# First stage of a decoder block on one core: where the first activation rows and the first columns of w_ada land, in which order their loads are issued, and a modulation summed in two halves

## The chip, the cores and the metric

One NeuronCore of one Trainium2 chip runs the whole kernel. Its five engines each work through their own instruction list in order and wait for one another by semaphores: TensorE (PE), VectorE (DVE), ScalarE (ACT), GpSimd (POOL) and SyncE (SP), whose instructions here are nearly all transfers between the chip's main memory and the core's SBUF. The metric is the device time of one execution in microseconds (us), as a median over runs.

## The reference, cut to what matters

One layer of a decoder with 1024 tokens of width 1024. The part that the change touches is the beginning, the first norm with its modulation:

```python
cond = jax.nn.silu(c)
mod = cond @ w_ada[l] + b_ada[l]
sh_a, sc_a, gt_a, sh_f, sc_f, gt_f = jnp.split(mod[:, None, :], 6, axis=-1)
h = rms_norm(x, norm_mix_g[l]) * (1.0 + sc_a) + sh_a
proj = h @ w_in[l]
```

`w_ada` is 1024 x 6144. Its first 2048 columns give the shift `sh_a` and the scale `sc_a` that the first norm needs. Everything behind `proj` (an attention branch, an mLSTM branch, their gated merge, then a squared-ReLU MLP) is the same before and after the change and takes all but the first 60 us or so of the run.

## The kernel before, in words

The 1024 tokens are eight tiles `j` of 128 rows. For each tile there are the steps `x_square` (load `xt`, 128 x 1024 in fp32, 512 KB, and sum its squares on ACT), `x_rms` (the power -0.5 on DVE and POOL), `x_turn` (scale the rows on DVE, transpose the tile on PE against the identity `ident`) and `x_out` (copy the transposed halves out of PSUM into `xT`, one half by ACT, one by DVE). A loop over `j` runs these staggered: tile `j` is squared while tile `j-1` is turned and tile `j-2` copied out.

Beside it `load_mod(q, j)` loads rows `j*128` to `j*128+127` of the first 2048 columns of `w_ada` for half `q` of the features (`wa`, two stretches of 512 columns, 512 KB) and adds `wa * cond` into an accumulator `macc` on DVE: one `tensor_scalar` for `j` = 0 and seven `scalar_tensor_tensor` after it. When all eight are in, `modulate(q)` sums `macc` over its 128 partitions by eight small matmuls against a matrix of ones and adds the bias (`shg`), from which `gsc` is made. The steps that `modulate` returns then apply scale and shift to `xT` and split the result into a rounded part `hh` (ACT) and the rest `hl` (DVE), which together are `hT`. `first_unit` multiplies `hT` by the first weights of `w_in` (`w_hi`, `w_lo`; PSUM tile `ops`) and by a small matrix of gate columns (`wgs`, PSUM tile `gps`). Half 0 of the features goes first; while its steps run, the eight `load_mod(1, j)` are woven in between.

In the loop's pass `j == 2` a set of small parameters is loaded: 67 rows of gains and biases into `parr` (five loads, from 0.5 to 24 KB), the two other constant matrices into `ksq` (`ones` is one of them), the gate columns `wg` (32 KB in pieces of 32 bytes) and two bias rows `gb`. PE turns `parr` into columns `par`; ACT and DVE make `wgs` out of `wg`.

What sets the order: a scheduler at build time lays every engine's list out; instructions wrapped in `pin(...)` keep the order in which the program states them among themselves. All loads of this stage are issued by SP, in SP's list order. Each load is given one of eight completion counters in rotation (DMAHW0 to DMAHW7), and a load whose counter still has an unfinished load on it holds SP up until that one has landed, so SP has at most eight loads under way. Tiles come from pools with a fixed number of buffers per tag: "v" and "e" have four each, "x" has four large ones of 128 x 8 x 512.

## Time and profile before

| | |
|---|---|
| median of 3 runs | 2036.21 us (2036.16 to 2036.49) |
| profiled execution, its own time | 2033.65 us |
| span of its trace | 2031.9 us |
| PE busy | 1970.7 us, 97% |
| DVE busy | 1636.7 us, 81% |
| ACT busy | 1053.0 us, 52% |
| moved by DMA | 307.21 MB |

The span is the stretch from the first to the last recorded instruction. Times in the trace count from the start of the span. In rows of the timeline the two first numbers are start and duration in us, then come engine, line of the kernel, operation, the tile written and the tile read, shapes and a count; a bracket gives how long the engine had been idle before the row and what released it. SPq is SP's list of transfers: its rows are the issue of a transfer, not its landing. The view of windows gives busy time of each engine in a stretch, then the granted TensorE clock (1.00 is full), the share of the DMA engines and GB/s.

### The profile page before, as it was taken

The numbers are of one execution on the slowest core, as the hardware profiler recorded it, in microseconds if no ns is written. First come the engines' busy times: TensorE is split into PE (matmuls) and PEld (weight loads), VectorE is DVE, ScalarE is ACT, GpSimd is POOL, SyncE is SP. The second block draws the span as 40 slices with busy tenths as digits, with TensorE's granted clock in tenths as the row PEclk, the third lists the DMA queues.
The fourth block names the chain that finished last, engine by engine and source line by source line (L and its number), as shares of the span: only waits on it lengthen the run. The fifth ranks groups of instructions, "written<-read, shape, count | busy, mean of one in ns | idle before, by whom it ended". The sixth has DMA issues, their size and how long they took to land.

```text
span 2031.9 us, 30206 instructions
## 1 busy us (share of the span) xinstructions
PE 1970.7 (97%) x11193; PEld 1709.9 (84%) x11193; DVE 1636.7 (81%) x2883; ACT 1053.0 (52%) x1983; POOL 55.8 (3%) x150
## 2 busy tenths in 40 slices
PE   5999999999999999999999889999999999999999
PEld 5999998888888899999999668877788888888887
DVE  7977668988766568999978757999867668999896
ACT  5523224544566557777766534546645545433332
POOL 0000000000011000000000100000000000000000
PEclk7999999999999999999999999999999999999999
DMA  8376633335665442322223875603446446755531
GB/s 285 107 221 205 203 113 119 104 104 181 194 169 170 121 116 63 84 63 84 63 83 87 288 263 186 202 22 127 147 145 218 165 151 227 276 181 156 165 114 73
DMA packets 205386, 307.21 MB, mean 151 GB/s; under 512 B 14435, under 2 KB 115454, under 8 KB 205238
## 3 DMA queue, kind: packets, MB, share of 16 engines
q1 hardware_dynamic: 202358, 295.84, 45.9%
q0 software_dynamic: 2880, 9.44, 1.2%
q8 instruction: 88, 1.44, 0.3%
q14 instruction: 60, 0.49, 0.1%
HBM read 212.19 MB, written 84.64 MB: 146 GB/s over the span
## 4 chain that ended last, share of the span: by engine, by line
PE 77%; DVE 8%; DMA 6%; issue 4%; ACT 4%; POOL 1%; SPq 0%; DVEq 0%; POOLq 0%; ACTq 0%
PE cps L329 18%; PE pa L329 10%; PE pc L329 10%; PE pb L329 10%; PE pd L329 5%; PE ps L167 4%; PE ps L166 4%; PE ps L168 4%; PE lg L1220 3%; PE pv L1273 2%; DMA ex<-ea_d 1%; PE ops L586 1%; PE tp L1253 1%; DMA w<-in_w_ff_dram 1%; DMA xt<-in_x_dram 1%
## 5 line engine op out<-in xcount | busy, mean ns | idle before, releaser
L329 PE MATMUL cps<-t_op,s_op 128*128 128x512 f32 x2016 | 466.8, 393 | 2.1 <-DVE t_op L139 1.8
L329 PEld LDWEIGHTS cps<-t_op,s_op 128*128 128x128 f32 x2016 | 377.9, 188 | 88.1 <-DVE t_op L139 2.1
L321 ACT ACTIVATE w_op<-w_st 128x512 fp32r<-128x512 f32 (+1 forms) x197 | 135.9, 705 | 196.2 <-PE pb L329 60.0
L139 DVE TENSOR_TENSOR w_op<-w_st,w_op 128x512 fp32r<-128x512 f32 (+1 forms) x197 | 150.0, 780 | 27.2 <-ACT w_op L321 25.3
L166 PE MATMUL ps<-w_hi,hT 128*128 128x256 f32 x512 | 146.5, 286 | 0.0
L167 PE MATMUL ps<-w_lo,hT 128*128 128x256 f32 x512 | 145.9, 285 | 0.0
L168 PE MATMUL ps<-w_hi,hT 128*128 128x256 f32 x512 | 145.6, 284 | 0.0
L321 ACT ACTIVATE s_op<-act 128x1024 fp32r<-128x1024 f32 x56 | 59.0, 1053 | 149.0 <-PE cps L329 109.5
L1230 ACT ACTIVATE ee<-ee,mneg 128x256 f32<-128x256 f32 (+7 forms) x128 | 98.4, 770 | 12.8 <-DVE mneg L1226 12.5
L1220 PE MATMUL lg<-kb,qe 128*128 128x512 f32 (+3 forms) x384 | 96.0, 357 | 5.2 <-DVE mneg L1226 3.5
L329 PE MATMUL pc<-bt,w_op 128*128 128x512 f32 x384 | 96.7, 399 | 2.4 <-ACT w_op L321 1.4
L167 PEld LDWEIGHTS ps<-w_lo,hT 128*128 128x128 f32 x512 | 97.6, 191 | 1.4 <-issue 0.9
L166 PEld LDWEIGHTS ps<-w_hi,hT 128*128 128x128 f32 x512 | 97.6, 191 | 0.5
L168 PEld LDWEIGHTS ps<-w_hi,hT 128*128 128x128 f32 x512 | 97.6, 191 | 0.3
L329 PE MATMUL pa<-b,w_op 128*128 128x512 f32 x384 | 93.5, 393 | 0.3 <-DVE w_op L139 0.3
L329 PEld LDWEIGHTS pc<-bt,w_op 128*128 128x128 f32 x384 | 71.8, 190 | 22.3 <-DVE w_op L139 5.3
L329 PEld LDWEIGHTS pa<-b,w_op 128*128 128x128 f32 x384 | 72.2, 189 | 15.6 <-DVE w_op L139 0.7
L317 DVE TENSOR_TENSOR acc<-cps,acc 128x512 f32<-128x512 f32 x108 | 71.5, 682 | 11.0 <-PE cps L329 11.0
L1226 DVE CUSTOM_DVE_ANT_0 ee<-lg,bs 128x512 f32<-128x512 f32 (+4 forms) x128 | 69.7, 558 | 8.8 <-PE lg L1220 7.8
L139 DVE TENSOR_TENSOR s_op<-act,s_op 128x1024 fp32r<-128x1024 f32 x56 | 68.2, 1218 | 6.6 <-ACT s_op L321 6.5
L1220 PEld LDWEIGHTS lg<-kb,qe 128*128 128x128 f32 x384 | 60.2, 189 | 14.3 <-DVE mneg L1226 8.5
L329 PE MATMUL pa<-hT,w_op 128*128 128x512 f32 x264 | 64.1, 392 | 0.0
(416 smaller groups left out, 4746.1 us busy)
## 6 DMA issues: line engine op xcount, KB each, us to landing
w_st<-in_w_in_dram SPq DMA_DIRECT2D x72, 512.0 KB, 4.0
act<-act_d SPq DMA_DIRECT2D x56, 512.0 KB, 4.3
w_st<-in_w_ff_dram SPq DMA_DIRECT2D x36, 512.0 KB, 4.1
crow<-in_w_ada_dram SPq DMA_DIRECT2D x32, 512.0 KB, 4.6
w<-in_w_ff_dram SPq DMA_DIRECT2D x32, 512.0 KB, 4.7
act_d<-s SPq DMA_DIRECT2D x40, 256.0 KB, 2.0
act_d<-c SPq DMA_DIRECT2D x33, 256.0 KB, 2.0
act_d<-m SPq DMA_DIRECT2D x33, 256.0 KB, 2.0
```

The source lines that it names most:

```text
L139: return (nc.gpsimd if pool else nc.vector).tensor_tensor(dst, src, hi.bitcast(F32), op=ALU.subtract)
L166: nc.tensor.matmul(o, lhsT=ah, rhs=bh, start=first, stop=False)
L167: nc.tensor.matmul(o, lhsT=ah, rhs=bl, start=False, stop=False)
L168: nc.tensor.matmul(o, lhsT=al, rhs=bh, start=False, stop=last)
L317: (nc.gpsimd if pick(pool, n) else nc.vector).tensor_tensor(o, a, b, op=ALU.add)
L321: nc.scalar.activation(dst[0], src, AF.Copy)
L329: nc.tensor.matmul(ps, lhsT=p, rhs=q, start=first and k == 0 and r == 0, stop=k == 3 and r == 2, skip_group_check=True,)
L586: nc.tensor.matmul(o, lhsT=a[ra], rhs=w[rb][:, k, :], start=k == 0 and ra == rb and j % 2 == 0, stop=k == KT - 1 and ra == 1, skip_group_c ...
L1220: nc.tensor.matmul(lg[:, 0:max(256, w)], lhsT=hd["q"][hf][e][:, r, q4 * P:(q4 + 1) * P], rhs=hd["k"][e][:, c0:c0 + max(256, w)], start=r = ...
L1226: nc.vector.tensor_tensor_reduce(ee[:, c0:c0 + w], lg[:, 0:w], hd["bs"][:, n - c0 - w:n - c0][:, ::-1], -0.125, first, ALU.add, ALU.min, last,
L1230: nc.scalar.activation(ee[:, 0:n], ee[:, 0:n], AF.Exp, bias=mneg[:, e:e + 1], scale=-1.0, accum_out=ssum[:, e:e + 1])
L1273: nc.tensor.matmul(pv[:, 0:256], lhsT=pts[kk // 4][r][:, (kk % 4) * P:(kk % 4 + 1) * P], rhs=v, start=kk == 0 and r == 0, stop=kk == qi an ...
```

## The change

The tiles `xt` are no longer taken one by one from the tag "v". Two large tiles of the pool of `hT` are taken ahead of `hT`, and each holds four of the eight tiles of x side by side. The eight loads of `wa` for half 0 get a buffer each (four of "e", four of "v"), and so do those for half 1 after them. Loading is taken out of `x_square` and `load_mod` into `x_load` and `fetch_mod`, all of it pinned, and stated ahead of the loop: x of tiles 0 to 3, then in turns `wa` and x of tiles 4 to 7, then the last four `wa`. `modulate` does its eight matmuls in two groups of four, each with its own bias addition and its own `gsc`.

```diff
+    xst = [xp.tile([P, KT, 512], F32, name=f"xst{i}", tag="x").rearrange("p k c -> p (k c)") for i in range(2)]
     hT = ActX("hT")
...
+    def x_load(j):
+        xs[j] = xst[j // 4][:, j % 4 * D:(j % 4 + 1) * D]
+        pin(nc.sync.dma_start(xs[j], x2[j * P:(j + 1) * P, :]))
+
     def x_square(j):
-        xt = xs[j] = wt("v", [P, D], "xt")
-        nc.sync.dma_start(xt, x2[j * P:(j + 1) * P, :])
+        xt = xs[j]
...
+    def fetch_mod(q, j):
+        was[q, j] = wt("ev"[j % 2], [P, 2, 512], "wa")
+        src = w_ada[0, j * P:(j + 1) * P, 0:2048].rearrange("p (s c) -> p s c", s=2)
+        pin(nc.sync.dma_start(was[q, j], src[:, :, q * 512:(q + 1) * 512]))
+
     def load_mod(q, j):
-        wa = wt("e", [P, 2, 512], "wa")
-        src = w_ada[0, j * P:(j + 1) * P, 0:2048].rearrange("p (s c) -> p s c", s=2)
-        nc.sync.dma_start(wa, src[:, :, q * 512:(q + 1) * 512])
+        wa = was.pop((q, j))
...
     def modulate(q):
-        ks = slice(q * 4, q * 4 + 4)
         mod = bank("pa", "mod")
-        for s in range(8):
-            nc.tensor.matmul(
-                mod[:, 2 * s:2 * s + 2], lhsT=mods[q][:, s // 4, (s % 4) * P:(s % 4 + 1) * P], rhs=ones[:, 0:2],
-                start=True, stop=True,
+
+        for k in range(0, 4, 2):
+            for s in (k, k + 1, 4 + k, 5 + k):
+                nc.tensor.matmul(
+                    mod[:, 2 * s:2 * s + 2], lhsT=mods[q][:, s // 4, (s % 4) * P:(s % 4 + 1) * P], rhs=ones[:, 0:2],
+                    start=True, stop=True,
+                )
+            kq = slice(q * 4 + k, q * 4 + k + 2)
+            nc.vector.tensor_tensor(
+                shg[:, :, kq], mod[:, 0:16].rearrange("p (s k r) -> p s k r", s=2, r=2)[:, :, k:k + 2, 0],
+                bada[:, 0:2, kq], op=ALU.add,
             )
-        nc.vector.tensor_tensor(
-            shg[:, :, ks], mod[:, 0:16].rearrange("p (s k r) -> p s k r", s=2, r=2)[:, :, :, 0],
-            bada[:, 0:2, ks], op=ALU.add,
-        )
-        nc.vector.scalar_tensor_tensor(gsc[:, ks], shg[:, 1, ks], 1.0, gmix[:, ks], op0=ALU.add, op1=ALU.mult)
+            nc.vector.scalar_tensor_tensor(gsc[:, kq], shg[:, 1, kq], 1.0, gmix[:, kq], op0=ALU.add, op1=ALU.mult)
...
     ada = [ada_unit(u) for u in range(8)]
+    for j in range(4):
+        x_load(j)
+    for j in range(4):
+        fetch_mod(0, j)
+        x_load(4 + j)
+    for j in range(4, NT):
+        fetch_mod(0, j)
     for j in range(NT + 3):
...
     ahead()
+    for j in range(NT):
+        fetch_mod(1, j)
     weave(modulate(0), [lambda j=j: load_mod(1, j) for j in range(NT)])
```

Three places of the engines' lists. The words in brackets name what an instruction waits for: DMAHW with a number is the completion counter of a load, an engine's name is that engine. First SP's list, from the third tile of x on, as it stood before:

```order
L500 DMA xt_150<-in_x_dram 128x1024
L101 DMA parr_169<-in_norm_mix_g_dram 8x128
L101 DMA parr_169<-in_b_ada_dram 48x128
L101 DMA parr_169<-in_norm_ffn_g_dram 8x128
L101 DMA parr_169<-in_mhn_g_dram 2x128 [waits DMAHW0_49]
L101 DMA parr_169<-in_subln_g_dram 1x128 [waits DMAHW1_49]
L1393 DMA ksq_87<-in_k_sq_dram 128x2x128 [waits DMAHW2_49]
L1396 DMA wg_180<-in_w_in_dram 128x8x8 [waits DMAHW3_49]
L1400 DMA gb_126<-in_b_igate_dram 128x4 [waits DMAHW4_49]
L1400 DMA gb_126<-in_b_fgate_dram 128x4 [waits DMAHW5_49]
L500 DMA xt_187<-in_x_dram 128x1024 [waits DMAHW6_49]
L526 DMA wa_206<-in_w_ada_dram 128x2x512 [waits DMAHW7_49]
```

and as it stands now, from the last tile of x on (`xst1` is the second large tile):

```order
L501 DMA xst1_108<-in_x_dram 128x1024 [waits DMAHW5_49]
L531 DMA wa_145<-in_w_ada_dram 128x2x512 [waits DMAHW6_49]
L531 DMA wa_147<-in_w_ada_dram 128x2x512 [waits DMAHW7_49]
L531 DMA wa_149<-in_w_ada_dram 128x2x512 [waits DMAHW0_49]
L531 DMA wa_151<-in_w_ada_dram 128x2x512 [waits DMAHW1_49]
L101 DMA parr_189<-in_norm_mix_g_dram 8x128 [waits DMAHW2_49]
L101 DMA parr_189<-in_b_ada_dram 48x128 [waits DMAHW3_49]
L101 DMA parr_189<-in_norm_ffn_g_dram 8x128 [waits DMAHW4_49]
L101 DMA parr_189<-in_mhn_g_dram 2x128 [waits DMAHW5_49]
L101 DMA parr_189<-in_subln_g_dram 1x128 [waits DMAHW6_49]
L1411 DMA ksq_87<-in_k_sq_dram 128x2x128 [waits DMAHW7_49]
L1414 DMA wg_200<-in_w_in_dram 128x8x8 [waits DMAHW0_49]
```

Before, the small parameters stood behind three tiles of x; now they stand behind all eight tiles of x and all eight `wa` of half 0. The counter DMAHW0 that `wg` waits for is held by `wa_149`, the seventh of the eight `wa`.

Second, ACT's list at the place where `wgs` is made, before:

```order
L502 ACTIVATE jk_152,ssx_115<-xt_150 128x1024 [waits DMAHW4_49]
L518 COPY xT00_118<-tp_138 128x4x128 [waits PE_49]
L1397 ACTIVATE wgs_181<-wg_180 128x8x8 [waits DMAHW3_49]
L502 ACTIVATE jk_189,ssx_115<-xt_187 128x1024 [waits DMAHW6_49,Activation_49]
L518 COPY xT00_118<-tp_155 128x4x128 [waits PE_49]
```

and now:

```order
L506 ACTIVATE jk_172,ssx_117<-xst0_107 128x1024 [waits DMAHW4_49]
L522 COPY xT00_120<-tp_160 128x4x128 [waits PE_49]
L1415 ACTIVATE wgs_201<-wg_200 128x8x8 [waits DMAHW0_49]
L506 ACTIVATE jk_207,ssx_117<-xst0_107 128x1024 [waits DMAHW5_49,Activation_49]
L522 COPY xT00_120<-tp_175 128x4x128 [waits PE_49]
```

The place is the same in both: `wgs` stands between the squares of tile 2 and tile 3. On DVE and PE too the instructions that read `wg` and `parr` stand where they stood, ahead of the scaling and the transposes of tile 2.

Third, DVE's list around `modulate(0)`, from the last but one `scalar_tensor_tensor` of half 0 on, before:

```order
L533 SCALAR_TENSOR_TENSOR macc_208<-wa_316,cond_97,macc_208 128x1024 [waits DMAHW1_49,DVE_49]
L533 SCALAR_TENSOR_TENSOR macc_208<-wa_319,cond_97,macc_208 128x1024 [waits DMAHW2_49,DVE_49]
L139 TENSOR_TENSOR w_lo_323<-w_st_324,w_hi_322 128x1024 [waits DMAHW3_49,Activation_49]
L543 TENSOR_TENSOR shg_116<-mod_332,par_170 128x2x4 [waits PE_49]
L547 SCALAR_TENSOR_TENSOR gsc_117<-shg_116,par_170 128x4 [waits DVE_49]
L139 TENSOR_TENSOR w_lo_323<-w_st_328,w_hi_322 128x1024 [waits DMAHW4_49,Activation_49]
L531 TENSOR_SCALAR macc_348<-wa_346,cond_97 128x1024 [waits DMAHW5_49]
L139 TENSOR_TENSOR hT10_108<-xT00_118,hT00_107 128x2x256 [waits Activation_49]
L533 SCALAR_TENSOR_TENSOR macc_348<-wa_354,cond_97,macc_348 128x1024 [waits DMAHW6_49,DVE_49]
L139 TENSOR_TENSOR hT10_108<-xT00_118,hT00_107 128x2x256 [waits Activation_49]
```

and now:

```order
L139 TENSOR_TENSOR w_lo_317<-w_st_318,w_hi_316 128x1024 [waits DMAHW3_49]
L542 SCALAR_TENSOR_TENSOR macc_224<-wa_151,cond_97,macc_224 128x1024 [waits DMAHW1_49,DVE_49]
L139 TENSOR_TENSOR w_lo_317<-w_st_322,w_hi_316 128x1024 [waits DMAHW4_49,Activation_49]
L554 TENSOR_TENSOR shg_118<-mod_342,par_190 128x2x2 [waits PE_49]
L558 SCALAR_TENSOR_TENSOR gsc_119<-shg_118,par_190 128x2 [waits DVE_49]
L554 TENSOR_TENSOR shg_118<-mod_342,par_190 128x2x2 [waits PE_49]
L558 SCALAR_TENSOR_TENSOR gsc_119<-shg_118,par_190 128x2 [waits DVE_49]
L540 TENSOR_SCALAR macc_358<-wa_326,cond_97 128x1024 [waits DMAHW6_49]
L139 TENSOR_TENSOR hT10_110<-xT00_120,hT00_109 128x2x256 [waits Activation_49]
L542 SCALAR_TENSOR_TENSOR macc_358<-wa_328,cond_97,macc_358 128x1024 [waits DMAHW1_49,DVE_49]
L139 TENSOR_TENSOR w_op_608<-w_st_586,w_op_608 128x1024 [waits DMAHW1_49,Activation_49]
L139 TENSOR_TENSOR hT10_110<-xT00_120,hT00_109 128x2x256 [waits Activation_49]
```

One of the two `w_lo` (1024 columns) has moved ahead of the last accumulation into `macc`, and the second ahead of `shg`. The `w_op`, which stood behind all accumulations of half 1, now stands ahead of the second subtraction for `hT`; ACT's rounding of the same `w_op` has moved likewise, ahead of the second rounding of `hT`. On PE the second group of four `mod` matmuls waits for DVE.

More of the change, by code (lines that the diff above doesn't have):

```diff
@@ L520, in x_out @@
             ))
+    was = {}
+    def fetch_mod(q, j):
+        was[q, j] = wt("ev"[j % 2], [P, 2, 512], "wa")
+        src = w_ada[0, j * P:(j + 1) * P, 0:2048].rearrange("p (s c) -> p s c", s=2)
+        pin(nc.sync.dma_start(was[q, j], src[:, :, q * 512:(q + 1) * 512]))
     def load_mod(q, j):
-        wa = wt("e", [P, 2, 512], "wa")
-        src = w_ada[0, j * P:(j + 1) * P, 0:2048].rearrange("p (s c) -> p s c", s=2)
-        nc.sync.dma_start(wa, src[:, :, q * 512:(q + 1) * 512])
+        wa = was.pop((q, j))
         if j == 0:
```

## The prediction

> **What bounds the kernel now.** I read the shares of the page first, then the stretch that the change touches.
>
> ```profile
> PE 1970.7 (97%) x11193; PEld 1709.9 (84%) x11193; DVE 1636.7 (81%) x2883; ACT 1053.0 (52%) x1983; POOL 55.8 (3%) x150
> PE   5999999999999999999999889999999999999999
> ```
>
> TensorE is busy 97% of the span, and of the 40 slices only the first (0 to 50.8 us) is half empty. The edit lies in that slice, so the stage that ends with PE's unbroken run is what counts. The view of windows shows where that run begins.
>
> ```profile
> 15.00:20.00 5.00, 1.30 (x8) 0.90 (x8) 4.18 (x8) 2.77 (x6) 1.10 (x2) 0.79 1.03 407
> 20.00:25.00 5.00, 3.65 (x16) 3.14 (x16) 4.95 (x8) 2.98 (x7) 1.10 (x2) 0.50 1.04 397
> 40.00:45.00 5.00, 4.92 (x21) 4.40 (x21) 5.00 (x6) 4.90 (x11) 0.00 (x0) 0.50 0.70 206
> 45.00:50.00 5.00, 5.00 (x36) 4.10 (x36) 5.00 (x7) 4.91 (x11) 0.00 (x0) 0.98 0.88 279
> ```
>
> From 45 us on PE is busy for the whole window, at full clock (0.98); before 40 us it is not, and from 20 to 45 us its clock is granted at half speed. In 15 to 25 us DVE is nearly full (4.18 and 4.95 of 5 us), and the transfers run at 407 and 397 GB/s. So behind 15 us DVE and the transfers bind. The chain that ends last names the links:
>
> ```profile
> 9.14 4.66 DMA xt<-in_x_dram
> 13.89 1.16 ACT jk L502 x2
> 33.84 3.56 PE mod L539 x16
> 37.88 1.10 ACT xT L560 x2
> 42.21 4.46 PE ops L586 x24
> ```
>
> x of tile 3 and its squares, the eight `mod` matmuls, the first modulation on ACT, and from 42.21 us only PE. Whatever moves 42.21 moves the end, so I work out that time.
>
> **The change, part by part.** The place where it decides is not x or `wa` but the small loads that now stand behind them. Before, they went out early:
>
> ```profile
> 3.40 0.34 SPq L101 DMA_DIRECT2D parr<-in_b_ada_dram  x1
> 6.93 0.39 SPq L1396 DMA_DIRECT2D wg<-in_w_in_dram  x1
> 10.11 0.26 ACT L1397 ACTIVATE wgs<-wg 128x64 fp32r<-128x64 f32 x1
> 15.74 0.74 DVE L531 TENSOR_SCALAR macc<-wa,cond 128x1024 f32<-128x1024 f32 x1
> 18.57 1.28 DVE L533 SCALAR_TENSOR_TENSOR macc<-wa,cond,macc 128x1024 f32<-128x1024 f32 x1
> 19.76 0.75 DVE L511 TENSOR_SCALAR xt<-xt,ssx 128x1024 f32<-128x1024 f32 x1
> 20.61 0.68 DVE L518 COPY xT<-tp 128x512 f32<-128x512 f32 x1
> 21.21 1.28 DVE L533 SCALAR_TENSOR_TENSOR macc<-wa,cond,macc 128x1024 f32<-128x1024 f32 x1
> 20.65 1.94 PE L514 MATMUL tp<-ksq,xt 128*128 128x128 f32 x8 [2.15 <-DVE xt L511]
> ```
>
> `wg` was issued at 6.93, and ACT made `wgs` at 10.11 without a wait. ACT's list, like DVE's and PE's, still has the readers of `wg` and `parr` ahead of the work on tile 2 or 3. Those engines take their lists in order, so squares of tiles 3 to 7, scalings of tiles 2 to 7 and all eight accumulations stand behind `wg`.
>
> *When does `wg` land now?* The rows are two of ACT's, one of SP's waits, and two of the view of transfers from 0 to 60 us (slices of 1.5 us; the last number of the last row is the time from issue to landing).
>
> ```profile
> 5.66 1.06 ACT L502 ACTIVATE jk<-xt 128x1024 bf16<-128x1024 f32 x1 [1.75 <-DMA xt<-in_x_dram]
> 8.28 1.06 ACT L502 ACTIVATE jk<-xt 128x1024 bf16<-128x1024 f32 x1 [0.19 <-DMA xt<-in_x_dram]
> ...
> SPq L1396 <- DMA xt<-in_x_dram: 0.9, 1, 0.9
> ...
> GB/s 0 87 232 410 376 117 20 75 352 377 406 425 397 403 395 396 389 389 385 365 348 371 385 385 355 37 0 198 201 288 244 299 291 307 275 39 0 0 0 11
> parr<-in_b_ada_dram SPq DMA_DIRECT2D x1, 24.0 KB, 5.1
> ```
>
> (a) ACT starts on the first x at 5.66 and on the third, released by its landing, at 8.28: 1.31 us for each 512 KB, 400 GB/s; from 12 to 36 us the slices hold 348 to 425. (b) SP really stops on a full set of counters: it held `wg` for 0.9 us until a tile of x had landed. (c) A 24 KB load (`b_ada`, issued at 3.40) took 5.1 us, until 8.5, just behind the third x at 8.28: small loads do not overtake. In the new list x and `wa` make 16 loads of 512 KB. The first lands at 5.66, the fifteenth (`wa_149`, whose counter `wg` needs) at 5.66 + 14 x 1.31 = 24.0, the sixteenth at 25.3. `wg` is issued at 24.0 and not sooner whatever the queue does. It cannot land before the 128 KB of `ksq`, which stand behind the sixteenth: 25.3 + 0.33 = 25.6. In the run before the geometry was the same (one 512 KB load and `ksq` still ahead), and it was there 3.2 us after issue (10.11 - 6.93) at the latest: 27.2. I take **26.8**, nearer that row. At 425 GB/s all through, the fifteenth would land 1.1 us sooner, at 365 GB/s 1.8 us later. Nothing below 25 is left, since 15 loads must be in.
>
> By the Trainium skill ("DMA: Bandwidth & Descriptors", Specifications) a core's share of main memory is about 358 GB/s; the 16 loads would then take 23.4 us instead of 21.0 and the sum below would be 2.4 us higher, an estimate from that page. This trace moves 397 to 407 GB/s in 15 to 25 us, so I stay with the trace.
>
> *From `wg` to the second accumulation.* `wgs` on ACT is done at 27.0, the squares of tile 3 take 1.16, to 28.15. Then DVE copies tile 1 (0.68) and starts the first accumulation at 28.85 (0.74), the scaling of tile 3 at 29.5 (0.75) and the copy of tile 2 at 30.35 (0.68; tile 2 is scaled by 28.2, and its transposes take 1.94, to 30.2), and the second accumulation at 30.95. Before it was at 18.57. From there DVE is the limit in both, 2.64 us a tile (21.21 - 18.57); that x and `wa` are all there no longer helps. **Shift so far +12.4.** The early loads of x are worth nothing in it: tile 3 no longer waits for its transfer (4.66 in the chain), but for `wg`.
>
> *Around `mod`.*
>
> ```profile
> 31.14 2.60 DVE L533 SCALAR_TENSOR_TENSOR macc<-wa,cond,macc 128x1024 f32<-128x1024 f32 x2
> 33.65 1.22 DVE L139 TENSOR_TENSOR w_lo<-w_st,w_hi 128x1024 fp32r<-128x1024 f32 x1
> 37.62 0.16 DVE L547 SCALAR_TENSOR_TENSOR gsc<-shg,par 128x4 f32<-128x4 f32 x1
> 37.71 1.22 DVE L139 TENSOR_TENSOR w_lo<-w_st,w_hi 128x1024 fp32r<-128x1024 f32 x1
> 39.67 0.69 DVE L139 TENSOR_TENSOR hT<-xT,hT 128x512 fp32r<-128x512 f32 x1
> ```
>
> Before, the two `w_lo` (1.22 each, some 1.1 where the next instruction overlaps the end) ran beside the `mod` matmuls and behind `gsc`. Now one stands ahead of the last accumulation, nothing hides it: **+1.1**. The last accumulation, which ended at 33.74 (31.14 + 2.60), ends at 33.74 + 12.4 + 1.1 = 47.25, and `mod` starts at 47.35 (33.84 before). The first four matmuls take half of 3.56, to 49.1, the first `gsc` is there at 49.5, 2.15 us behind the start of `mod` where it was 3.94 (37.78 - 33.84). But the second group waits for DVE's first `shg` (0.25), its `gsc` comes at 51.5, and DVE runs the first accumulation of half 1 (0.74) and `hT`'s first subtraction (0.69, to 52.8) only after it. ACT's second modulation waits for it too (1.10, 51.55 to 52.65).
>
> *The moved `w_op`.*
>
> ```profile
> 52.55 1.06 ACT L321 ACTIVATE w_op<-w_st 128x1024 fp32r<-128x1024 f32 x1 [1.38 <-DMA w_st<-in_w_in_dram]
> 53.65 1.22 DVE L139 TENSOR_TENSOR w_op<-w_st,w_op 128x1024 fp32r<-128x1024 f32 x1 [0.56 <-ACT w_op L321]
> ...
> w_st<-in_w_in_dram SPq DMA_DIRECT2D x4, 512.0 KB, 6.9
> ```
>
> Before, its rounding on ACT (1.06) and subtraction on DVE (1.22) fell into gaps, with 1.38 and 0.56 us of idle time before them. Now they stand ahead of the second `hT` parts: ACT 52.6 to 53.65, rounding of `hT` to 54.25; DVE second accumulation from 52.7 (1.28), `w_op` 53.9 to 55.1, subtraction of `hT` to 55.7. Its load waits until the first `w_lo` has freed a buffer (46.1); with the 6.9 us that such loads took it lands at 53.0, so at most 0.4 us more. PE's unbroken run starts at 55.75: 8.4 us behind the start of `mod`, just as before (42.21 - 33.84 = 8.37). Pairing gains about 1.1 us, the moved `w_op` loses it: **0**, between -1.1 (if `w_op` were hidden) and +0.4.
>
> *Later.*
>
> ```profile
> 54.55 1.84 PE L539 MATMUL mod<-ksq,macc 128*128 128x2 f32 x16
> ```
>
> For half 1 the second group of `mod` again waits for DVE, now on PE's own path: **+0.25**. DVE's rest of half 1, six accumulations and six subtractions, takes 6 x (1.28 + 0.69) = 11.8 us at most, to 67.5; PE reaches `mod` 12.3 us after the start of its run (54.55 - 42.21), at 68.1. So DVE's work stays hidden, by 0.6 us.
>
> *Clock.*
>
> ```profile
> 44.09 0.41 PE L586 MATMUL ops<-w_lo,hT 128*128 128x256 f32 x1
> 44.73 0.41 PE L586 MATMUL ops<-w_lo,hT 128*128 128x256 f32 x1
> 45.32 0.28 PE L586 MATMUL ops<-w_lo,hT 128*128 128x256 f32 x1
> 45.68 0.28 PE L586 MATMUL ops<-w_lo,hT 128*128 128x256 f32 x1
> ```
>
> Three matmuls of 256 columns lie between each two of these rows: 0.21 us for one at half speed, 0.12 at full. The rise came near 45.1, 2.9 us into the unbroken run, and PE had worked for most of the 2.5 us ahead of it. Now it works in bits between 51.4 and 55.7. If the rise comes up to 2.5 us later in the run, that costs up to 2.5 x (1 - 0.12/0.21) = 1.1; I take **+0.3**, nearer to no difference.
>
> The page "TensorE: Matmul & The Clock Gate" of the Trainium skill (Part 1) gives full speed after about 3.4 us of sustained work, by a free-running window. By it the rise would come some 3.4 us into the run instead of 2.9, +0.2 as an estimate; the rise in this trace, 2.9 us into the run and 5.4 us behind PE's first matmul of the stage, does not contradict it.
>
> **Sum:** 12.4 + 1.1 + 0 + 0.25 + 0.3 = 14.05. The profiled execution, 2033.65 us around a span of 2031.9, becomes 2047.7 around 2045.9. The median lies 2.6 above that execution: 2036.2 + 14.05 = **2050.3**.
>
> **Rivals.** *A: The small loads stall nothing*, because they overtake the large ones. Then `wgs` is made near 10.1 as before, tile 3 (landed at 5.66 + 3 x 1.31 = 9.6) is squared by 11.5, the first accumulation runs at 12.3 and the second 2.1 later at 14.4 instead of 18.57; less the exposed `w_lo` the gain is 4.2 - 1.1 = 3.1, time 2033.1. For it speaks that x of tile 3 and the fourth load behind it do wait in the chain now; against it row (c), and row (b) above all, since a load that SP has not issued cannot overtake. 4%.
>
> *B: The delay is taken up later.* PE is idle for 61 us of the span (2031.9 - 1970.7). If 10 to 13 us of this were waits for transfers that run ahead on their own, these would shrink, and 1 to 4 us would be left: 2037 to 2040. Against it, PE's waits from 38 to 200 us:
>
> ```profile
> PE ops L586 <- ACT hT L563: 2.3, 1, 2.3
> PE pc L329 <- DVE m L317: 1.2, 1, 1.2
> ```
>
> These two are all of them, neither is for a transfer, and later loads wait for buffers that this same chain frees. 4%.
>
> *C: The transfers are slower with eight always under way.* At the 365 GB/s of the slower slices 1.8 us more; a late clock and a late `w_op` load add up to 0.8 and 0.4: 2053.3. For it speaks that the slices with `wa` alone are the slow ones (348 to 385 from 30 to 36 us). 12%. The 358 GB/s of the page named above lie on this side.
>
> *D: `wg` lands at its lower bound* (25.6 instead of 26.8) behind loads at 425 GB/s, and `w_op` is hidden: -1.2 - 1.1 - 1.1, 2046.9. 10%.
>
> **How the numbers follow.** Forecast 70%, D 10%, C 12%, A 4%, B 4%. C and D carry the ends of the unknown costs; PE's later waits (2.3 and 1.2 us in the rows) can shrink or grow by some 2 us more, so the range is **2045 to 2055**. Within 0.2%, 4.1 us, a time of this kernel cannot be told from no change: B falls there, and A lies 1.0 us inside the bound, so half of its chance goes to each side of it. Faster 0.02, same 0.06, slower 0.92.
>
> **What would show it.** In the profile after: `wgs` on ACT at 26 to 27.5 with some 15 us idle before it, released by the load of `wg`; the first accumulation near 29, the second 2.1 us later and then one each 2.64; `mod` near 47.3; `w_op` on ACT between the first two roundings of `hT`; PE unbroken from about 55.7. Wrong if `wgs` runs before 20, if the accumulations come closer than 2.6 us, or if PE's unbroken run starts 13 us later but the end does not.

## The result, and the profile after

| | before | after |
|---|---|---|
| median | 2036.85 us (2036.16 to 2043.02, 6 runs) | 2049.49 us (2046.65 to 2052.18, 6 runs) |
| ratio | | 1.0057, interval 1.0041 to 1.0072 |
| profiled execution, its own time | 2033.65 us | 2050.73 us |
| span of its trace | 2031.9 us | 2049.0 us |

The changed kernel is 12.6 us slower, 0.6%. The page of the kernel after begins as that of before did, with one slice changed: the first one of 40 fell from 5 to 3 tenths of PE.

```profile
PE 1975.1 (96%) x11193; PEld 1712.1 (84%) x11193; DVE 1636.9 (80%) x2887; ACT 1052.4 (51%) x1983; POOL 57.0 (3%) x150
PE   3999999999999999999999889999999999999999
```

The view of windows shows what fills that slice (busy time of PE, PEld, DVE, ACT, POOL, then clock, DMA share and GB/s). The clock column is no guide here: this profile has no record of the clock before 58.1 us, and the view prints 1.00 where there is none, though the matmuls up to that time run at half speed (their rows stand further down).

```profile
15.00:20.00 5.00, 0.00 (x0) 0.00 (x0) 0.00 (x0) 0.00 (x0) 0.00 (x0) 1.00 1.04 399
20.00:25.00 5.00, 0.00 (x0) 0.00 (x0) 0.00 (x0) 0.00 (x0) 0.00 (x0) 1.00 1.04 381
...
55.00:60.00 5.00, 4.97 (x27) 4.56 (x28) 5.00 (x6) 4.91 (x11) 0.00 (x0) 1.00 0.01 2
```

For ten microseconds no engine computes anything, while the transfers run at 399 and 381 GB/s. Before, DVE was busy for 9.13 of these ten. The chain that ends last names what everything waits for:

```profile
13.40 10.47 DMA wa<-in_w_ada_dram
23.89 2.59 DMA wg<-in_w_in_dram
...
46.42 1.85 PE mod L549 x8
...
55.02 4.47 PE ops L597 x24
```

SP stands until the seventh `wa` has landed, issues `wg`, and 2.59 us later the stage begins to move. PE's unbroken run starts at 55.02 us instead of 42.21: 12.8 us later, and the medians lie 12.6 us apart. The rows of the timeline show the three engines at the readers of the small loads and what follows.

```profile
23.89 0.39 SPq L1414 DMA_DIRECT2D wg<-in_w_in_dram  x1
26.15 0.34 PE L107 MATMUL tp<-ksq,parr 67*128 67x67 f32 x1 [14.06 <-DMA parr<-in_subln_g_dram]
26.50 0.26 ACT L1415 ACTIVATE wgs<-wg 128x64 fp32r<-128x64 f32 x1 [16.35 <-DMA wg<-in_w_in_dram]
26.53 0.23 DVE L108 COPY par<-tp 128x67 f32<-128x67 f32 x1 [15.42 <-PE tp L107]
28.49 0.74 DVE L540 TENSOR_SCALAR macc<-wa,cond 128x1024 f32<-128x1024 f32 x1
30.49 1.28 DVE L542 SCALAR_TENSOR_TENSOR macc<-wa,cond,macc 128x1024 f32<-128x1024 f32 x1
43.90 1.22 DVE L139 TENSOR_TENSOR w_lo<-w_st,w_hi 128x1024 fp32r<-128x1024 f32 x1
45.04 1.28 DVE L542 SCALAR_TENSOR_TENSOR macc<-wa,cond,macc 128x1024 f32<-128x1024 f32 x1
```

Idle times of 14.06, 16.35 and 15.42 us, on PE, ACT and DVE, end within 0.4 us of each other. PE and ACT stand at readers of `parr` and `wg`, some 30 KB each, and DVE at the copy of what PE makes of `parr`.

The stage is told. Two things the trace did not settle: which of the three readers costs what, and why the same instruction at the end of the program lies 17.1 us behind its place before, where 100 to 500 us into it the distance was 13.1 to 13.5 us (found by pairing each DVE instruction of one trace with the same one of the other).

### The profile page after: what moved, and what is told of

Read it like the earlier page. It is cut to its first block, busy times and chain, and to the rows that moved or that the text cites. A ratio compares the mean times of both kernels' runs of the same rounds, so it can differ in the third digit from the quotient of the medians.

```text
span 2049.0 us, 30208 instructions
## 1 busy us (share of the span) xinstructions
PE 1975.1 (96%) x11193; PEld 1712.1 (84%) x11193; DVE 1636.9 (80%) x2887; ACT 1052.4 (51%) x1983; POOL 57.0 (3%) x150
## 4 chain that ended last, share of the span: by engine, by line
PE 73%; DVE 10%; DMA 7%; issue 6%; ACT 3%; POOL 1%; SPq 0%; POOLq 0%; DVEq 0%; ACTq 0%
PE cps L329 17%; PE pc L329 10%; PE pb L329 9%; PE pa L329 9%; PE pd L329 5%; PE ps L167 3%; PE ps L168 3%; PE ps L166 3%; PE lg L1231 3%; PE pv L1284 2%; DMA ex<-ea_d 2%; PE tp L1264 1%; DMA w<-in_w_ff_dram 1%; DMA wa<-in_w_ada_dram 1%; DVE s_op L139 1%
## 5 line engine op out<-in xcount | busy, mean ns | idle before, releaser
L1241 ACT ACTIVATE ee<-ee,mneg 128x256 f32<-128x256 f32 (+7 forms) x128 | 98.3, 770 | 12.6 <-DVE mneg L1237 12.3
L329 PE MATMUL pc<-t,w_op 128*128 128x512 f32 x264 | 64.1, 391 | 0.0
```

The costliest lines, as they stand in the source:

```text
L329: nc.tensor.matmul(ps, lhsT=p, rhs=q, start=first and k == 0 and r == 0, stop=k == 3 and r == 2, skip_group_check=True,)
L1241: nc.scalar.activation(ee[:, 0:n], ee[:, 0:n], AF.Exp, bias=mneg[:, e:e + 1], scale=-1.0, accum_out=ssum[:, e:e + 1])
```

## The experiments

Theory S is the prediction's: nothing of the transfers costs in itself; three engines reach the readers of late small loads in their lists, and stand. Rival L: the large tiles tie the tiles of x to one another, or sixteen loads at once cost by themselves. Rival O: the moved `w_lo` and `w_op` and the two groups of `modulate` cost the time.

**How many large loads stand ahead.** In the first two runs the nine small loads are issued behind three large loads (where they were before) and behind eight, instead of behind sixteen. The readers stay between tiles 2 and 3.

```diff
+    loads = [lambda j=j: x_load(j) for j in range(4)]
+    for j in range(4):
+        loads += [lambda j=j: fetch_mod(0, j), lambda j=j: x_load(4 + j)]
+    loads += [lambda j=j: fetch_mod(0, j) for j in range(4, NT)]
+    run(loads[:3])          # second run: loads[:8]
+    par, gmix, bada, gffn, mhg, subg, wg, wgs = par_loads()
+    run(loads[3:])
```

> The changed kernel with one thing put back: the nine small loads (parr, ksq, wg, gb) are issued behind the third tile of x, as before the change, and not behind all sixteen loads of 512 KB. Large tiles for x, own buffers for wa and the summing in two groups stay. Theory S (engines stand still for the late small loads): wgs on ACT runs near 10 us instead of 26.5, the fourth x is issued near 9.1 and lands near 13.5, PE's unbroken run starts at 41 to 43 us instead of 55.0, time 2034 to 2038. Rival L (the two large tiles tie the tiles of x together, a reader of one waits for the loads of its three neighbours): the run starts near 55 still, time near 2049. Rival O (the moved w_lo and w_op and the second group's wait for DVE cost the time): w_lo and w_op are not ahead here, the wait for DVE is, so some 2 us less than the changed kernel, 2047.

> The same, but the nine small loads are issued behind eight loads of 512 KB instead of sixteen (as changed) or three (as before). Theory S: wg is held until the seventh of them has landed (5.6 + 6 x 1.31 = 13.5) and lands 2.6 us later as it did in the changed kernel, so wgs near 16.1, 10.4 us sooner than 26.5; w_op is not moved ahead here (1.2 us less), w_lo is; PE's unbroken run starts near 43.5, time 2049.5 - 11.6 = 2038, between 2036.5 and 2040. Rival L and rival O: no change from the small loads' place, 2047 to 2050.

With three loads ahead: 2039.31 us against 2036.73, ratio 1.0012 (0.9996 to 1.0027). With eight: 2040.27, 1.0016 (1.0001 to 1.0031). ACT's row of `wgs` with eight loads ahead:

```profile
15.81 0.26 ACT L1422 ACTIVATE wgs<-wg 128x64 fp32r<-128x64 f32 x1 [6.41 <-DMA wg<-in_w_in_dram]
```

So `wgs` runs at 9.36, 15.81 and 26.50 us with 3, 8 and 16 large loads ahead, about 1.3 us a load, close to the 1.31 us that the prediction read for 512 KB. In both runs the stage came as expected, and the end 1.3 and 0.3 us above the latest time that I had given (2038 and 2040). PE's unbroken run starts at 42.15, 43.68 and 55.02. From 8 to 16 loads the one moves by 10.7 us and the other by 11.3. From 3 to 8 the run moves by 1.5 only, because with three loads ahead something else was late, and ACT's rows of that kernel show it:

```profile
9.36 0.24 ACT L1422 ACTIVATE wgs<-wg 128x64 fp32r<-128x64 f32 x1
...
13.36 1.06 ACT L506 ACTIVATE jk<-xst 128x1024 bf16<-128x1024 f32 x1 [3.29 <-DMA xst<-in_x_dram]
```

The fourth tile of x stands behind the nine small loads on SP and lands at 13.3. Either the small loads are late or that tile is; only one of them is on the path. Rival L falls with these two runs: with the same tiles and the same sixteen loads PE's run starts 11 to 13 us earlier. (Part of it, 1 to 2.5 us, is that the list of the second kernel moves only `w_lo` and that of the first neither `w_lo` nor `w_op`.)

**The two groups.** `modulate` with all eight matmuls in one group, in the changed kernel; and the kernel before with two groups and nothing else.

```diff
-        for k in range(0, 4, 2):
-            for s in (k, k + 1, 4 + k, 5 + k):
+        for s in range(8):
```

> The changed kernel without the two groups: modulate sums eight matmuls at once again. Everything else, the small loads' place and the moved w_lo and w_op too, is as in the changed kernel. Theory S: the stall stays, wgs at 26.5; the first gsc comes 1.8 us later, the second 0.25 sooner, PE's wait for DVE in half 1 (0.25) goes; start of the unbroken run 55.0 to 56.1, time +0 to +1 on the changed kernel, 2049 to 2051. Rival O, as far as it lays the time on the groups: several us faster, 2040 to 2046.

The end: 2054.19 us against 2036.73, 1.0085 (1.0065 to 1.0104), above the 2049 to 2051 that I expected. PE's run too starts later than expected, at 56.58 instead of 56.1 at the latest; half a microsecond of it is there before `mod`, which starts at 46.94 (46.42 with two groups), since `wgs` came at 26.97. What follows is the surer reading: the run starts 9.64 us behind `mod`. With two groups it was 8.60 behind, before the change 8.37. Two rows of DVE in this kernel:

```profile
52.77 0.69 DVE L139 TENSOR_TENSOR hT<-xT,hT 128x512 fp32r<-128x512 f32 x1 [1.22 <-ACT hT L572]
...
54.70 1.23 DVE L139 TENSOR_TENSOR w_op<-w_st,w_op 128x1024 fp32r<-128x1024 f32 x1
```

The moved `w_op` is still there, ahead of the second subtraction for `hT`, and costs 9.64 - 8.37 = 1.3 us; the two groups take 9.64 - 8.60 = 1.0 back. Both were put at 1.1 in the prediction. Rival O could explain 1 to 2 us of the 12.8, not the rest.

> The kernel before with only the two groups in modulate; loads and tiles as before. DVE has a w_lo between the second shg and its gsc here. Theory S: wgs at 10.1, the first gsc 1.8 us sooner, the second 1.4 later (0.25 for the wait, 1.15 for w_lo); the unbroken run starts within 41.5 to 43.5, time 2035.5 to 2038, no clear difference from before. Rival O: slower by several us, 2040 or more.

2039.1 us, 1.0013 (0.9999 to 1.0027), no clear difference, though above the 2038 that I had given as the latest. The groups alone do not even help where they are meant to: PE's run starts at 43.13, 0.9 us later than before. DVE's rows and a wait of PE:

```profile
38.23 0.16 DVE L545 TENSOR_TENSOR shg<-mod,par 128x4 f32<-128x4 f32 x1 [1.76 <-PE mod L540]
38.72 1.23 DVE L139 TENSOR_TENSOR w_lo<-w_st,w_hi 128x1024 fp32r<-128x1024 f32 x1 [0.33 <-issue]
39.86 0.15 DVE L549 SCALAR_TENSOR_TENSOR gsc<-shg,par 128x2 f32<-128x2 f32 x1
...
41.33 0.80 PE L588 MATMUL ops<-w_hi,hT 128*128 128x256 f32 x2 [2.17 <-DVE hT L139]
```

Here the scheduler put the second `w_lo` between the second `shg` and its `gsc`; PE gets its first operand early, and then waits 2.17 us for the next. In the changed kernel both `w_lo` stand ahead of `shg`, and the groups gain. What an edit is worth depended on which list the scheduler built around it.

**The readers, not the loads.** If theory S holds, the loads may stay late, if only nobody stands at their readers.

```diff
-            par.turn()
...
-            nc.scalar.activation(wgs[:, :, 0:8], wg, AF.Copy)
-            nc.vector.tensor_tensor(wgs[:, :, 8:16], wg, ...)
...
+    par.turn()              # behind the loop over the tiles
+    nc.scalar.activation(wgs[:, :, 0:8], wg, AF.Copy)
+    nc.vector.tensor_tensor(wgs[:, :, 8:16], wg, ...)
```

> The loads in the order of the change, all sixteen large ones ahead of the nine small ones, but the instructions that read the small loads (the transpose of parr, the copy par, and wgs on ACT and DVE) stand behind the loop over the tiles instead of between tiles 2 and 3. All of the computation is done.
> Theory S (what costs is that three engines reach the readers early and stand there): the squares of tiles 3 to 7 and the accumulations run as x and wa come in. First accumulation near 12, second near 14 (28.49 and 30.49 with the change). wg still lands at 26 to 27. ACT now has the rounding w_hi, whose weights are loaded behind the small loads, ahead of the square of tile 7, and so stands until 29.5 to 30.5; the last accumulation ends near 40 instead of 45 to 46, mod starts near 40 (46.42 with the change, 33.84 before), PE's unbroken run at 47 to 48.5 (55.02 with the change). Time 2041 to 2044.
> Rival (the lateness of the small loads costs wherever they are read, for instance through the transfers queued behind them): run start stays at 54 to 56, time 2048 to 2051.

2044.16 us against 2035.17, 1.0044 (1.0032 to 1.0057), and PE's run from 49.41: 5.6 us earlier than with the change, by moving the readers of `parr` and `wg` alone. (1.1 of it is the `w_lo`, which this list hides beside `mod`.) The loads were issued in the order of the change. What is left is the same thing at another place, on ACT first and behind it on DVE:

```profile
17.87 1.06 ACT L506 ACTIVATE jk<-xst 128x1024 bf16<-128x1024 f32 x1 [1.02 <-DMA xst<-in_x_dram]
...
30.94 1.06 ACT L153 ACTIVATE w_hi<-w_st 128x1024 fp32r<-128x1024 f32 x1 [11.92 <-DMA w_st<-in_w_in_dram]
...
14.46 1.28 DVE L542 SCALAR_TENSOR_TENSOR macc<-wa,cond,macc 128x1024 f32<-128x1024 f32 x1
...
33.55 0.15 DVE L510 TENSOR_SCALAR ssx<-ssx 128x1 f32<-128x1 f32 x1 [11.89 <-ACT jk L506]
```

The second accumulation ran at 14.46 instead of 30.49. Then ACT stood 11.92 us at `w_hi`, whose weights are loaded behind the small loads, and the square of tile 7 stood behind it. The wait that was removed made room for the next one in the list, as expected; it ended at 30.94, half a microsecond later than the latest that I had given, and PE's run began 0.9 later.

**Small loads from another queue.** The nine small loads are issued by ACT at the start of its list; tiles and loads of x and `wa` as in the change; one group.

```diff
+            pin(nc.scalar.dma_start(self.rows[r:r + n, 0:src.shape[-1]], src))
...
-            pin(nc.sync.dma_start(wg, w_in[0][:, C_MG:C_MG + 8]...))
+    pin(nc.scalar.dma_start(wg, w_in[0][:, C_MG:C_MG + 8]...))   # ahead of the loads of x
```

> The large tiles and the loads of x and wa as in the change, but the nine small loads are issued by ACT at the start of its list instead of by SP behind the sixteen large ones, and modulate sums all eight slices in one group as before. All of the computation is done.
> Theory S: the readers no longer wait behind anything; wgs is made by 10, the first accumulation near 12, the second near 14, after that one each 2.5 us, so the last ends near 29, mod starts near 29.5 (33.84 before), PE's unbroken run at 37.5 to 39 (42.21 before). If all of it reaches the end, 3 to 4.5 us less than before: 2032 to 2034 beside 2036.7.
> Rival 1 (the large tiles or the sixteen loads at once cost something of their own): wgs early, but the accumulations no earlier than before (second near 18.6 or later), time 2036 to 2040.
> Rival 2 (small loads are held up by large ones on whatever queue): wgs at 20 or later, time 2042 or more.

> The kernel with the small loads on ACT's queue, large tiles and one group once more, unaltered: its first stage was 1.9 us shorter than before, and its median 4.6 us longer, though all instruction lists behind the first stage are the same.
> If the later loss belongs to this kernel: run start near 40.3 again, median 2038 to 2041, and in the profile 4 us or more lost between 100 us and the end.
> If it is scatter of the later stages: median 2034 to 2036, and the loss is not there again or lies elsewhere.

First: 2039.81 us against 2035.17, 1.0017 (1.0005 to 1.0029). Again: 2039.57 against 2035.85, 1.0018 (1.0003 to 1.0033). In the stage theory S holds: `wgs` at 10.73, the second accumulation at 16.85 (18.57 before), PE's run from 40.34 and 40.46, 1.9 and 1.8 us earlier than before. It is less than the 3.2 to 4.7 us that I expected, for a reason of which ACT's list shows one half, and the chain that ends last the other:

```profile
3.66 0.76 ACTq L503 DMA_DIRECT2D gb<-in_b_igate_dram  x1
5.82 0.35 ACTq L503 DMA_DIRECT2D gb<-in_b_fgate_dram  x1
6.20 1.28 ACT L511 ACT_TABLE_LOAD   x1 [6.20 <-DMA xst<-in_x_dram]
...
7.61 1.04 ACT L532 ACTIVATE jk<-xst 128x1024 bf16<-128x1024 f32 x1
```

```profile
5.82 6.00 DMA gb<-in_b_fgate_dram
11.84 7.69 DMA xst<-in_x_dram
19.61 1.15 ACT jk L532 x2
```

ACT too was held, by its ninth load, until a tile of x had landed, and its first square came at 7.61 instead of 5.66. But it also went the other way: in this trace the loads of both engines take the same eight counters in turn, so small loads of ACT held SP. The ninth, 2 KB of `gb`, took 6.00 us to land, and only then, at 11.84, could SP issue a tile of x whose squares are on the chain. The holds had moved, they were not gone. The page "DMA: Bandwidth & Descriptors" of the Trainium skill ("Issuing engines are not separate DMA queues") says that loads from several engines run on the same sixteen DMA engines, and that only issue time is saved. Here that was worth much: what SP holds back until 23.89 us has not been issued, and `wgs` came 15.8 us earlier. But the rest of the expectation failed: by the ratios the end is 3.5 and 3.7 us later than before although the stage is shorter. (The time lies in the range of rival 1, but its sign in the stage, a second accumulation at 18.6 or later, did not come.) What can be said of that is below, with the next two runs and at the end.

**What is left when both are taken out, and the queue alone.** First the large tiles and the order of the loads, with the small loads at their old place and one group; then the kernel before with nothing changed but the nine loads on ACT's queue.

> The large tiles, a buffer for each wa and the stated order of the loads, with the nine small loads behind the third tile of x as in the kernel before and all eight mod matmuls in one group as before: what is left of the change when late small loads and the two groups are taken out. All of the computation is done.
> Theory S: wgs near 9.4, second accumulation near 18.4 (18.57 before), mod near 33.6 (33.84 before), gsc 3.8 later, PE's unbroken run near 42 (42.21 before); the end within 1 us of before, 2035 to 2037. The +0.85 that the same loads with two groups showed at the start of PE's run comes then from the groups.
> Rival (the large tiles and buffers cost later, behind the first stage): run start near 42, but the end 2 to 3 us above before, 2037.5 to 2039.

2038.66 us against 2035.85, 1.0006 (0.9988 to 1.0024): no difference that can be told. PE's run starts at 42.41 (42.21 before), and 100 to 300 us into the program the instructions lie 0.1 to 0.3 us behind those of before. Large tiles and early loads alone gain nothing, since the nine small loads hold tile 3 as they did before; they cost nothing in the stage either. Whether they cost something later is not settled: the interval reaches from 2.4 us less to 4.9 us more, and the median lies in the range that I had given for the rival.

> The kernel before with one edit: its nine small loads are issued by ACT at the start of its list. x and wa keep their old tiles, loads and order; modulate is one group. All of the computation is done.
> Stage: tile 3 of x no longer stands behind nine small loads on SP; second accumulation at 15 to 17.5 (18.57 before), PE's unbroken run at 39.5 to 41.5 (42.21 before).
> If issuing loads from a second queue is what costs later: the end 2 us or more above before, 2037.5 to 2041, like the kernel with large tiles and ACT's queue. If the later loss comes with the large tiles and the other rotation of buffers: 2033 to 2036.5, the gain of the stage reaches the end.

2041.88 us, 1.0028 (1.0013 to 1.0042). The stage was misjudged: PE's run starts at 43.38, 1.2 later than before, since a tile of x, issued at 14.1 by the chain, landed only at 20.4. The end is 5.7 us later by the ratio, and 0.8 of it is there at 100 us. So the later loss of the kernels with ACT's queue does not need the large tiles.

**The change and the kernel before, once more.**

> The change once more, unaltered, to have it on the same chip and in the same rounds as the two variants, and with a second profile. Both theories: 2048 to 2051, wgs at 26 to 27, PE's unbroken run at 54.5 to 55.5. If the further 2 to 3.5 us that its first profile lost between 500 and 700 us belong to the change, they are there again against a second profile of the kernel before; if they are scatter of the first profile of before, they are not.

> The kernel before once more, unaltered, for a second profile of it. Scatter: between 500 and 700 us its instructions lie 2 to 3.5 us behind those of the first profile, and its own time is 2036 to 2038. A cost of the change: they lie within 0.5 us of the first profile.

The change: 2053.51 us against 2035.17, 1.0088 (1.0071 to 1.0104), above the 2048 to 2051 that both theories gave. Its stage is the same to 0.2 us (`wgs` at 26.53, PE's run from 55.22), but the clock rose later. PE's rows, first of the first profile of the change, around the rise:

```profile
57.54 0.41 PE L597 MATMUL ops<-w_lo,hT 128*128 128x256 f32 x1
57.75 0.56 PE L597 MATMUL ops<-w_hi,hT 128*128 128x256 f32 x2
58.15 0.28 PE L597 MATMUL ops<-w_lo,hT 128*128 128x256 f32 x1
```

and of its second profile:

```profile
60.51 0.63 PE L607 MATMUL gps<-hT,wgs 128*16 128x512 f32 x1
60.93 0.46 PE L611 MATMUL gps<-hT,wgs 128*8 128x512 f32 x1
61.23 0.40 PE L607 MATMUL gps<-hT,wgs 128*16 128x512 f32 x1
61.46 0.40 PE L611 MATMUL gps<-hT,wgs 128*8 128x512 f32 x1
```

In the first, a matmul of 256 columns takes 0.21 us from start to start ahead of the rise and 0.12 behind it; in the second, matmuls of 512 columns come 0.42, then 0.30, then 0.23 us apart. So the rise came at 58.1 in the one and at 61.1 in the other, 3.1 and 5.9 us into the run (3.0 before). `mod` of half 1 starts at 67.35 and 68.79: of these 1.4 us, 0.2 are the later run and 1.2 the later clock.

The second profile lost another 1.5 us at 126 us, behind PE's wait for `m`. The windows there, first of the first profile, then of the second:

```profile
126.00:128.00 2.00, 2.00 (x19) 2.00 (x18) 1.43 (x3) 0.00 (x0) 0.00 (x0) 1.00 0.85 274
```

```profile
126.00:128.00 2.00, 2.00 (x10) 2.00 (x11) 2.00 (x4) 0.00 (x0) 0.00 (x0) 0.50 0.77 231
```

PE waits for `m` for 1.8 and 1.9 us (1.2 before). In the second profile the granted clock then stands at 0.50, and sixteen matmuls take 0.21 us each instead of 0.12: 1.5 us.

The kernel before: its second profile (2033.55 us) lies within 0.9 us of the first throughout (by the median of each 100 us), and 0.1 at the end. So the further loss that all profiles of variants show behind 100 us is not the chance of one profile of before. For the change it is 3.6 and 4.0 us (13.5 to 17.1, and 16.5 to 20.5). Of this, 3.4 us of the first profile and 1.2 of the second fall between 500 and 700 us, in the mLSTM part, where PE waits for short chains over ACT and DVE; so the 2 to 3.5 us asked about were not there again in full. PE's waits there, before:

```profile
PE num L166 <- ACT sw L960: 2.1, 3, 0.9
PE lps L683 <- DVE mcol L676: 1.5, 1, 1.5
```

and in the first profile of the change:

```profile
PE num L166 <- ACT sw L971: 4.7, 3, 2.1
PE lps L694 <- DVE mcol L687: 2.2, 1, 2.2
```

All waits of PE in that stretch sum to 10.6 us before (9.8 in the second profile) and to 12.4 and 11.8 with the change. The instruction lists are the same there, and the granted clock of the stretch is 0.97 or 0.98 in all four profiles. But both profiles of before lie 1.6 to 3.2 us under its medians, whose single runs spread from 2031.7 to 2049.5 us, so part of these 3.6 and 4.0 us is that the two profiles of before are quick ones. How much, and what sets it, stays open.

All runs at a glance. "At 100 us" is how far the instructions 100 to 200 us into the program lie behind those of the first profile of before, "end" is the ratio times 2036 us, and "later" the difference of the two; the intervals of the ratios reach 2.4 to 4 us to either side, so single numbers of the two last columns are rough.

| kernel | `wgs` | PE's run | at 100 us | end | later |
|---|---|---|---|---|---|
| the change | 26.50 | 55.02 | +13.5 | +11.6 | -1.9 |
| the change again | 26.53 | 55.22 | +16.5 | +17.9 | +1.4 |
| 3 large loads ahead | 9.36 | 42.15 | +0.8 | +2.4 | +1.6 |
| 8 large loads ahead | 15.81 | 43.68 | +2.8 | +3.3 | +0.5 |
| one group | 26.97 | 56.58 | +14.9 | +17.3 | +2.4 |
| groups alone | 10.50 | 43.13 | +2.6 | +2.6 | 0.0 |
| readers behind the loop | 33.42 | 49.41 | +7.0 | +9.0 | +2.0 |
| large tiles alone | 9.54 | 42.41 | +0.1 | +1.2 | +1.1 |
| ACT's queue | 10.73 | 40.34 | -1.8 | +3.5 | +5.3 |
| ACT's queue again | 10.92 | 40.46 | -1.3 | +3.7 | +5.0 |
| ACT's queue, old tiles | 10.70 | 43.38 | +0.8 | +5.7 | +4.9 |

No version here beats the kernel before.

## Why the prediction was right, step by step

- *`wg` lands at 26.8.* Issued at 23.89 (24.0 predicted), landed and read at 26.5. The reason was right in each part: SP held by the counter of the seventh `wa`, no overtaking (the sixteenth large load landed at 25.4, `ksq` at 26.2). The runs with 3 and 8 loads ahead give the same 1.3 us a load.
- *Three engines stand at the readers.* Shown by moving the readers alone (5.6 us) and the loads alone (11 to 13 us). They stood 14.1 to 16.4 us, ACT 16.35; "some 15" was predicted for it.
- *Second accumulation at 30.95.* It came at 30.49.
- *One accumulation each 2.64 us.* **This was wrong**: after the first at 28.49 they started at 30.49, 33.01, 35.52 and 38.04, so each 2.51. I had named "closer than 2.6 us" as what would refute the forecast; what it refutes is the sentence that DVE is the limit in both kernels. DVE's rows of the kernel before and of the kernel after show where the 0.13 us lie:

```profile
19.76 0.75 DVE L511 TENSOR_SCALAR xt<-xt,ssx 128x1024 f32<-128x1024 f32 x1
20.54 0.15 DVE L506 TENSOR_SCALAR ssx<-ssx 128x1 f32<-128x1 f32 x1
```

```profile
34.20 0.75 DVE L515 TENSOR_SCALAR xst<-xst,ssx 128x1024 f32<-128x1024 f32 x1
34.86 0.15 DVE L510 TENSOR_SCALAR ssx<-ssx 128x1 f32<-128x1 f32 x1
```

Now `ssx` follows the scaling after 0.66 us, overlapping its end; before, after 0.78, since it waited for the squares of a tile of x that had just landed. A pair of x and `wa` takes 2 x 1.31 = 2.62 us to land: before, the transfers set the pace of 2.64, and DVE, nearly full, only looked like it. ACT's rows of before show it from the other side: the squares of these tiles start at 16.71, 19.36, 21.98 and 24.62, each released by the landing of its tile after 1.0 to 1.2 us of idle time. The runs agree: where DVE has to wait for x the pace is 2.6 (18.40 and 21.04 with three loads ahead, 14.46 and 17.07 with the readers behind the loop), where x is there in time 2.5 (20.28 and 22.80 with eight). The pace was 2.64 for three tiles only, so the error is small: 0.35 us in all. With the second accumulation 0.46 earlier and `w_lo` 0.1 cheaper it makes the 0.9 us by which `mod` started sooner than forecast, 46.42 instead of 47.35.
- *The exposed `w_lo`, +1.1.* It holds DVE for 45.04 - 43.90 = 1.14 us. The last accumulation starts 2.33 us behind the one before it, where it was 1.3: 1.0.
- *Pairing and the moved `w_op`, together 0.* The run starts 8.60 us behind `mod` instead of 8.37: +0.2. The kernel with one group gives the two terms apart, -1.0 and +1.3 (-1.1 and +1.1 predicted).
- *Second group of half 1, +0.25.* **This did not come.** The rows of half 1 in the kernel after:

```profile
67.35 0.95 PE L549 MATMUL mod<-ksq,macc 128*128 128x2 f32 x8
...
68.48 0.28 PE L597 MATMUL ops<-w_hi,hT 128*128 128x256 f32 x1
68.60 1.01 PE L549 MATMUL mod<-ksq,macc 128*128 128x2 f32 x8
```

Three matmuls of `ops` stand between the two groups in PE's list, and PE has no idle time there. It waited 0.26 us for DVE's `shg` in half 0 only, which is inside the 8.60 us above. Behind `mod` of half 1 the distance to before is 12.9 us, where it was 12.8 ahead of it: less than 0.1.

- *Clock, +0.3, at most 1.1.* 0 in the first profile, 1.2 in the second. The bound was a little too low: I let the rise come at most 2.5 us later in the run, and it came 2.9 later. That the clock could fall again behind the wait for `m`, 1.5 us in the second profile, was no term of the sum. The page "TensorE: Matmul & The Clock Gate" of the Trainium skill (Part 1) has a window of about 3.4 us that runs freely; as an estimate from it, a run that begins just inside a window can wait nearly two of them, 6.8 us. The rises in these kernels came 2.2 to 5.9 us into the run: all lie under that estimate, and the latest lies beyond the 5.4 us that my bound allows.
- *The sum.* 14.05 us predicted for the stage; the start of PE's run and the clock give 12.8 + 0 = 12.8 in the first profile and 13.0 + 1.2 = 14.2 in the second. At 100 to 200 us the traces show 13.5 and 16.5: 0.6 and 0.7 of that is PE's longer wait for `m`, for which the range had room, and 1.5 in the second is the clock behind it. So the stage came out 1.2 us shorter than the sum in the first profile and as long as the sum in the second, whose clock rose late. The medians moved by 12.6 and 18.3: the sum lies between them. That it comes so near is in part luck: what the sum has too much (0.9 at `mod`, 0.25 for the wait that did not come) stands against what it left out (the wait for `m` and the clock behind it).
- *Rivals.* A (small loads overtake) and B (the delay is taken up later) did not come: nothing was taken up, and behind the stage the profiles lost a little more. C and D were matters of size; the transfers ran at 399 and 381 GB/s, between the two.

## What to carry to other kernels

When loads are put in "order of use", use means the place in each engine's list at which the first reader stands, not the size or the importance of the data: here 66 KB (`parr` and `wg`) that three engines read early were put behind 8 MB. To cost such an edit, find the load on which the issuing engine will be held, add its landing, and follow each reader's list to see what stands behind it; here the start of PE's run came out 0.7 us from the forecast (55.02 and 55.75), while the medians of two measurements of the same kernel lay 4 us apart. A gain of 2 us in the first stage, read from the trace, was not a gain at the end: two microseconds have to be seen in the median, not only in the stage.

## What the runs showed of the hardware that was not expected

**Fewer matmuls in the same time, 300 us later.** In the three profiles with the nine small loads on ACT's queue, PE gets through fewer matmuls in a stretch where nothing stops it. The view of windows, first before and then with ACT's queue (the first bracket is the number of PE's matmuls):

```profile
300.00:490.00 190.00, 190.00 (x832) 155.79 (x831) 171.33 (x215) 93.81 (x130) 0.00 (x0) 1.00 0.35 114
```

```profile
300.00:490.00 190.00, 190.00 (x825) 154.75 (x824) 170.85 (x214) 93.21 (x129) 0.00 (x0) 1.00 0.33 114
```

832 and 825, at full clock in both, PE busy for all of it, and the same GB/s. The other two profiles with ACT's queue, one of them with the old tiles, have 825 and 824; all nine other profiles have 831 to 834. From start to start a matmul takes 228.9 ns before and 230.8 with ACT's queue, as a mean: stretches of some 15 to 50 matmuls with a mean near 232 ns alternate with stretches at 227. The slow ones hold some 44% of the matmuls before, and 69 to 84% with ACT's queue. The pattern repeats. Seven or eight matmuls in 190 us are 1.6 to 1.8 us of the 4.9 to 5.3 that these kernels lose behind the stage. The lists of PE, DVE, ACT and POOL are the same there, so it is not the work. That the loads do it is not shown: the same edit takes the tiles `gb`, `parr`, `wg` and `wgs` ahead of `hT`, so tiles may lie elsewhere in SBUF, and no run has the tiles so with the loads on SP. What sets the slow stretches stays open, and so does where the other 3 us go.
